# Both MLP products of a two-layer fp32 decoder as seven block products, with sums of weight blocks formed in DRAM by accumulating DMAs

## The chip, the cores and the metric

The kernel runs on one core of a Trainium2 chip. The metric is the device time of one execution in microseconds (us). Lower is better. Engines are named as the profile names them: PE (TensorE, the matrix engine), DVE (VectorE), ACT (ScalarE), POOL (GpSimd), SP (SyncE, which here only issues DMAs).

## The reference

One batch of 1024 tokens of 1024 features goes through two layers and a last RMSNorm, all in float32. The first layer mixes tokens by multi-head latent attention (MLA), the second by stick-breaking attention; each then has a cross-attention into 256 memory tokens and an MLP with 4096 hidden features:

```python
def sq_relu_mlp(h, w_in, w_out):
    return jnp.square(jax.nn.relu(h @ w_in)) @ w_out

def reference(x, mem, positions, ...):
    h = x
    for i in range(DEPTH):                       # DEPTH = 2
        a = rmsnorm(h, norm_mix[i])
        if i % 2 == 0: h = h + mla_mixer(a, cos, sin, ...)
        else:          h = h + stick_breaking_mixer(a, ...)
        h = h + mem_cross_attn(rmsnorm(h, norm_cross[i]), rmsnorm(mem, norm_mem[i]), ...)
        h = h + sq_relu_mlp(rmsnorm(h, norm_mlp[i]), mlp_w_in[i], mlp_w_out[i])
    return rmsnorm(h, norm_final)
```

## The kernel before

The residual stream `x` lies transposed in SBUF, features on partitions, as 16 tiles of 128 x 512: eight tiles of features for each of two chunks of 512 tokens. Every fp32 product is made of three passes in PE's faster format: an operand is split into `h` (rounded) and `l` (the rest), and `mm3` (L101 to L104) adds wh·xh, wh·xl and wl·xh into one PSUM bank. Weights come through `load_w` (L91 to L98): SP loads a raw block of 256 KB, ACT casts it to `h` (L97), POOL forms `l` (L89). Results leave PSUM through DVE or ACT.

Tiles are handed out from pools with a fixed number of slots for each tag, and a tile whose slots are all in use waits until one is free:

```python
SLOTS = dict(x=16, a=32, g=24, o=8, p=6, f=4, raw=3, w=8, pt=4, tmp=5)
PSLOTS = dict(s=3, pt=2, acc=3)
```

A scheduler orders the instructions of each engine by a simulated timeline; SP then issues all its DMAs in that order. A DMA queue has eight semaphores used in turn, so that an issue waits for the eighth DMA before it (`DMAHW..` in the order excerpts for SP's, `DMASW..` for POOL's).

The stages follow each other in time: MLA and the first cross-attention 0 to 617 us, the first MLP 617 to 1316, stick-breaking and cross-attention 1316 to 2037, the second MLP 2037 to about 2730, and then the last norm. In the attention stages `weave` (L257) emits two streams side by side: `self_attn` of one head, and as filling the projections of the next ones.

Before the MLP, `ready` takes each finished tile of `x`: it is multiplied by the gain alone and split (`gain_split`, tag `a`), and the statistics of the norm are gathered by `Norm`; `finish` of that class transposes and sums them (L138, L142) and spreads 1/rms over the partitions (L113, L114). Since 1/rms is a factor of each token, the first product of the MLP can begin without it: it is multiplied in when a bank is evicted (L854). Then the square of relu (L855) and the split of the result (L858, POOL). `win(f)` makes one f-tile of 128 hidden features for both chunks (2 x 8 k-tiles x 3 passes); after each four f-tiles ("a part", of eight) a product with four k-tiles of `w_out` is added onto `x` (`add_x`, L233). The last part of the second layer goes through `finish`, which also writes the output.

## Time and profile before

| | us |
|---|---|
| median of 3 runs | 2745.91 |
| lowest and highest run | 2743.05 and 2746.37 |
| profiled execution, its span | 2743.0 |
| PE busy | 2662.9 (97%) |
| DVE / POOL / ACT busy | 1373.9 / 1029.2 / 970.3 |
| the two MLP stages (617 to 1316, 2037 to 2743) | 699 and 706 |

The profiled execution's own time is its span, 2743.0 us, which is 2.9 us below the median of the runs. The page is read from the top: the busy shares name the engine that could bound the time, the slices say whether that holds in each stage, and the granted clock says whether PE ran at full speed. Then the waits of that engine say what is left besides its own work.

### The profile page before, as it was taken

Reading aid. Unit: us, or ns where it says so; the run is one execution under the profiler, and the core shown is the slowest. Engines: PE = TensorE matmul, PEld = TensorE weight load, DVE = VectorE, ACT = ScalarE, POOL = GpSimd, SP = SyncE. Lnnn points to the kernel's source line nnn. Section 1 sums busy time; section 2 is a strip of 40 time slices with the busy share of each in tenths; the row PEclk is TensorE's granted clock in tenths of the full one; section 3 lists DMA queues with packets and bytes.
Section 4 is the critical chain, followed back from the end, with each engine's and each line's share of the span. In section 5 each row is a group of like instructions: output and inputs, shape, how many; then the busy total and the mean of one; then the engine's idle time right before and its main releaser. Section 6 shows DMA issues by size and latency. Waiting matters only on the chain.

```text
span 2743.0 us, 34762 instructions
## 1 busy us (share of the span) xinstructions
PE 2662.9 (97%) x13446; PEld 2239.1 (82%) x13446; DVE 1373.9 (50%) x2504; ACT 970.3 (35%) x1956; POOL 1029.2 (38%) x788
## 2 busy tenths in 40 slices
PE   8899999999999999999999999999999999999997
PEld 6788889787888888888888888877878888888886
DVE  6777776874222222223475766687762222222227
ACT  7677676552111111112343333345531111111112
POOL 3543235544333333343423232246253333333332
PEclk9999999999999999999999999999999999999998
DMA  3000003111111111111111010122021111111111
GB/s 118 28 23 23 27 21 97 31 43 46 54 50 50 43 46 58 47 50 35 32 32 39 24 39 24 39 70 62 24 62 46 54 43 46 54 46 52 38 50 62
DMA packets 70164, 125.48 MB, mean 46 GB/s; under 512 B 7792, under 2 KB 12656, under 8 KB 70000
## 3 DMA queue, kind: packets, MB, share of 16 engines
q1 hardware_dynamic: 69856, 123.15, 15.1%
q8 instruction: 105, 1.72, 0.3%
q14 instruction: 59, 0.48, 0.1%
q10 hardware_dynamic: 144, 0.13, 0.0%
HBM read 119.05 MB, written 4.19 MB: 45 GB/s over the span
## 4 chain that ended last, share of the span: by engine, by line
PE 82%; DVE 12%; ACT 2%; issue 2%; POOL 1%; DMA 0%; SPq 0%; DVEq 0%; ACTq 0%; POOLq 0%
PE ps_acc L104 16%; PE ps_acc L103 16%; PE ps_acc L102 16%; PE ps_s L104 9%; PE ps_s L102 9%; PE ps_s L103 9%; PE ps_s L370 4%; DVE f L434 2%; PE ps_pt L392 2%; DVE a L192 2%; DVE p L439 1%; DVE x L233 1%; DVE tmp L131 1%; DVE tmp L181 1%; PE ps_s L775 1%
## 5 line engine op out<-in xcount | busy, mean ns | idle before, releaser
L89 POOL TENSOR_TENSOR w<-raw,w 128x512 fp32r<-128x512 f32 (+1 forms) x293 | 385.4, 1317 | 586.8 <-ACT w L97 567.0
L233 DVE TENSOR_TENSOR x<-ps_acc,x 128x512 f32<-128x512 f32 x408 | 278.1, 686 | 331.8 <-PE ps_acc L104 330.2
L97 ACT CAST w<-raw 128x512 fp32r<-128x512 f32 (+1 forms) x293 | 178.8, 611 | 438.4 <-PE ps_s L103 209.2
L102 PE MATMUL ps_acc<-a,w 128*128 128x512 f32 (+1 forms) x776 | 300.9, 388 | 10.1 <-DVE tmp L349 5.2
L104 PE MATMUL ps_acc<-a,w 128*128 128x512 f32 (+1 forms) x776 | 301.0, 388 | 1.0 <-POOL w L89 1.0
L103 PE MATMUL ps_acc<-a,w 128*128 128x512 f32 (+1 forms) x776 | 299.3, 386 | 1.6 <-DVE a L192 1.5
L89 POOL TENSOR_TENSOR g<-tmp,g 128x512 fp32r<-128x512 f32 x120 | 158.2, 1320 | 295.8 <-ACT g L184 237.3
L89 POOL TENSOR_TENSOR g<-pt,g 128x512 fp32r<-128x512 f32 x96 | 124.3, 1294 | 278.9 <-ACT g L858 278.9
L233 DVE TENSOR_TENSOR x<-ps_s,x 128x512 f32<-128x512 f32 x120 | 82.9, 691 | 228.1 <-PE ps_s L104 228.1
L858 ACT CAST g<-pt 128x512 fp32r<-128x512 f32 x96 | 59.5, 620 | 349.9 <-DVE pt L855 349.9
L102 PEld LDWEIGHTS ps_acc<-a,w 128*128 128x128 f32 x776 | 147.5, 190 | 39.7 <-DVE tmp L349 5.8
L854 DVE TENSOR_TENSOR pt<-ps_acc,tmp 128x512 f32<-128x512 f32 x64 | 44.1, 691 | 259.8 <-PE ps_acc L104 251.0
L103 PEld LDWEIGHTS ps_acc<-a,w 128*128 128x128 f32 x776 | 147.4, 190 | 31.9 <-DVE a L192 5.0
L104 PEld LDWEIGHTS ps_acc<-a,w 128*128 128x128 f32 x776 | 147.4, 190 | 30.1 <-POOL w L89 1.4
L89 POOL TENSOR_TENSOR p<-raw,p 128x512 fp32r<-128x512 f32 x73 | 97.2, 1331 | 175.6 <-ACT p L97 161.7
L854 DVE TENSOR_TENSOR pt<-ps_s,tmp 128x512 f32<-128x512 f32 x64 | 44.2, 691 | 236.9 <-PE ps_s L104 233.7
L104 PE MATMUL ps_s<-g,w 128*128 128x512 f32 (+1 forms) x378 | 148.2, 392 | 0.0
L102 PE MATMUL ps_s<-g,w 128*128 128x512 f32 (+1 forms) x378 | 148.0, 392 | 0.0
L103 PE MATMUL ps_s<-g,w 128*128 128x512 f32 (+1 forms) x378 | 148.0, 391 | 0.0
L102 PE MATMUL ps_acc<-g,f 128*128 128x512 f32 (+1 forms) x377 | 146.2, 388 | 0.0
L103 PE MATMUL ps_acc<-g,f 128*128 128x512 f32 (+1 forms) x377 | 146.2, 388 | 0.0
L104 PE MATMUL ps_acc<-g,f 128*128 128x512 f32 (+1 forms) x377 | 145.9, 388 | 0.0
(242 smaller groups left out, 7001.6 us busy)
## 6 DMA issues: line engine op xcount, KB each, us to landing
raw<-in_w_in SPq DMA_DIRECT2D x128, 256.0 KB, 2.6
raw<-in_w_out SPq DMA_DIRECT2D x128, 256.0 KB, 2.6
x<-in_xT SPq DMA_DIRECT2D x16, 256.0 KB, 5.1
raw<-in_w_mo SPq DMA_DIRECT2D x16, 256.0 KB, 2.7
raw<-in_w_xk SPq DMA_DIRECT2D x16, 256.0 KB, 2.7
raw<-in_w_xv SPq DMA_DIRECT2D x16, 256.0 KB, 2.7
raw<-in_w_xq SPq DMA_DIRECT2D x16, 256.0 KB, 2.6
raw<-in_w_xo SPq DMA_DIRECT2D x16, 256.0 KB, 2.6
```

Source lines behind the costliest of these rows:

```text
L89: eng.tensor_tensor(out=l, in0=full, in1=h.bitcast(F32), op=ALU.subtract)
L97: nc.scalar.copy(out=h, in_=raw)
L102: nc.tensor.matmul(out=ps, lhsT=wh, rhs=xh, start=start, stop=False, skip_group_check=True)
L103: nc.tensor.matmul(out=ps, lhsT=wh, rhs=xl, start=False, stop=False, skip_group_check=True)
L104: nc.tensor.matmul(out=ps, lhsT=wl, rhs=xh, start=False, stop=stop, skip_group_check=True)
L192: nc.vector.scalar_tensor_tensor(out=l, in0=xt, scalar=g, in1=h.bitcast(F32), op0=ALU.mult, op1=ALU.subtract)
L233: nc.vector.tensor_tensor(out=x[c][f], in0=ps, in1=x[c][f], op=ALU.add)
L370: nc.tensor.matmul(out=ps[:, :n], lhsT=lh, rhs=rh, start=(i == 0), stop=(i == len(passes) - 1), skip_group_check=True)
L392: nc.tensor.transpose(out=tp[:, o0:o0 + P], in_=col(probs[qi][kb // 4], kb % 4), identity=ident)
L434: nc.vector.tensor_tensor_scan(out=rev, data0=rev, data1=pt[j][:, :n], op0=ALU.mult, op1=ALU.bypass, initial=1.0 if j == len(pieces) - 1 e ...
L854: nc.vector.tensor_tensor(out=t, in0=ps, in1=r[c], op=ALU.mult)
L858: nc.scalar.copy(out=h, in_=t)
```

## The change

The matrices of each MLP are cut in two in both directions: the hidden product's tokens into the two chunks, its features into k-tiles 0 to 3 and 4 to 7, and the hidden features into parts. A product of 2 x 2 blocks is then made from seven block products instead of eight (Strassen's scheme, in Winograd's form), from four sums of weight blocks S1 to S4 and four sums of activation blocks T1 to T4. f-tiles 0 to 3 stay with the ordinary product; the other 28 form 14 pairs.

- **Weight sums.** `weight_sums(i)` forms S1 to S4 of both weight matrices of a layer in DRAM: `begin` copies a block (SP, L924 of the changed kernel), `add` adds another onto it by a DMA that accumulates (POOL's queue, L929). Each of the eight stages (begin S1, begin S3, add S1, begin S2 from S1, add S3, add S2, begin S4 from S2, add S4) has 12 DMAs of 7.34 MB together. They are emitted from `weave`, on two of three of its steps, in the layer's attention stage.
- **Entry.** For the MLP's norm `ready` now gathers the statistics first; when they are complete each tile is multiplied by gain and 1/rms (`normed`, DVE, tag `p`) and split (ACT, and DVE or POOL in turn). `quad(k)` forms T1 to T4 of the activations during the four ordinary f-tiles.
- **Input product.** `win` loads three raw weight tiles and four sums, splits all seven, and `seven` makes seven products of four k-tiles each in three PSUM banks, with an eviction (ACT or DVE) after each. The seven results that the next product needs, each 256 KB, are spilled to DRAM.
- **Output product.** `fetch` loads the seven tiles of a pair again and splits them; `wout` works on pairs 1, 2, 3, then 4 at a time, and 3, 2, 1 at the end, adds the results directly onto the tiles of `x`, and keeps one product (`p1`) per block until the end. The four ordinary f-tiles, also spilled, are reloaded and multiplied at the end.

Matmuls recorded before: 13446. The program of the change has 671 fewer.

```diff
+    def split(src, tag, eng):
+        w = src.shape[-1]
+        h, l = T(tag, F32R)[:, :w], T(tag, F32R)[:, :w]
+        nc.scalar.copy(out=h, in_=src)
+        split_l(l, src, h, eng)
+        return h, l
...
     def ready(c, f, gcol):
+        if gcol in (G_MLP, G_MLP + 8):
+            norm[c].add(x[c][f], nc.vector if f % 2 else nc.gpsimd)
+            if f == FT - 1:
+                rms[c], norm[c] = norm[c].finish(), Norm(D)
+                for k in range(FT):
+                    t = T("p")
+                    normed(t, c, k, gcol)
+                    act[c].append(split(t, "a", nc.vector if k % 2 else nc.gpsimd))
+            return
...
     def weave(main, fill):
         for n in mg:
+            turn[0] += 1
+            if turn[0] % 3 < 2:
+                next(aside[0], None)
...
+    def weight_sums(i):
...
+        def begin(name, src):
+            for key in keys:
...
+                tc.keep_in_program_order(nc.sync.dma_start(out=whole(name, *key), in_=src(*key)))
+                yield
+        def add(name, *src):
+            for key in keys:
+                tc.keep_in_program_order(nc.gpsimd.dma_start(out=whole(name, *key), in_=block(*key, *src),
+                                                             accum_op=ALU.add))
+                yield
...
+        yield from begin("S1", blk(1, 0))
+        yield from begin("S3", blk(0, 0))
+        yield from add("S1", 1, 1)
+        yield from begin("S2", other("S1"))
+        yield from add("S3", 1, 0)
+        yield from add("S2", 0, 0)
+        yield from begin("S4", other("S2"))
+        yield from add("S4", 0, 1)
+    def seven(a, b, n, psum, evict):
+        banks = [PS(psum) for _ in range(3)]
+        begun = set()
+        for (an, bn, j), ev in zip(SEVEN, evict):
+            wh, wl = a[an]
+            for k in range(n):
+                xh, xl = b[bn][k]
+                mm3(banks[j], col(wh, k), col(wl, k), xh, xl, j not in begun, k == n - 1)
+                begun.add(j)
+            ev(banks[j])
...
+        def win(n, kp):
...
+            for name, stage, tag, eng in (("A11", "raw", "w", po), ("S2", "p", "w", po), ("A12", "raw", "w", po),
+                                          ("S3", "p", "a", po), ("S1", "p", "a", po), ("A22", "raw", "a", po),
+                                          ("S4", "p", "a", po)):
+                t = T(stage)
...
+                nc.sync.dma_start(out=t, in_=src)
+                wa[name] = split(t, tag, eng)
...
+            seven(wa, b, 4, ("s", "acc")[n % 2], (e1, e2, e3, e4, e5, e6, e7))
...
+            for name, t in (("B11", g11), ("B21", g21), ("B22", g22), ("T1", t1), ("T3", g12), ("T2", t2), ("T4", t4)):
+                d = spilt[kp][name] = dram(f"{name}_{kp}")
+                nc.sync.dma_start(out=d, in_=t)
...
+        def fetch(kp):
+            r = ready_b[kp] = {}
+            for name, tag, eng in (("B11", "a", ve), ("T2", "g", po), ("B21", "a", ve), ("T3", "g", po),
+                                   ("T1", "g", ve), ("T4", "o", po), ("B22", "a", ve)):
+                t = T("tmp")
+                nc.sync.dma_start(out=t, in_=spilt[kp][name])
+                r[name] = split(t, tag, eng)
```

Where the change moves instructions, the order of the engines shows it at three places.

SP in the MLA stage, where the projections' weights are loaded. `uv`, `uqp`, `uk`, `uqn` and `mo` are weights of the MLA. Before:

```order
L95 DMA raw<-in_w_uv 128x512 [waits DMAHW4_49,Pool_49]
L95 DMA raw<-in_w_uqp 128x384 [waits DMAHW5_49,Pool_49]
L95 DMA raw<-in_w_mo 128x512 [waits DMAHW6_49,Pool_49]
L95 DMA raw<-in_w_mo 128x512 [waits DMAHW7_49,Pool_49]
L95 DMA raw<-in_w_uk 128x256 [waits DMAHW0_49,Pool_49]
L95 DMA raw<-in_w_uqn 128x384 [waits DMAHW1_49,Pool_49]
```

After, with S2 (`S_.._2789` and on) begun from the sums S1 (`S_.._1171` and on):

```order
L96 DMA raw<-in_w_uv 128x512 [waits DMAHW7_49,DMAHW4_49,Pool_49]
L96 DMA raw<-in_w_uqp 128x384 [waits DMAHW5_49,DMAHW0_49,Pool_49]
L924 DMA S_in_0_2789<-S_in_0_1171 32x4x2048 [waits DMAHW1_49,DMASW0_49]
L96 DMA raw<-in_w_mo 128x512 [waits DMAHW6_49,DMAHW2_49,Pool_49]
L924 DMA S_out_0_2848<-S_out_0_1221 32x2x2048 [waits DMASW1_49]
L924 DMA S_out_0_2888<-S_out_0_1242 32x2x2048 [waits DMASW2_49]
L924 DMA S_in_0_2961<-S_in_0_1280 32x4x2048 [waits DMASW3_49]
L924 DMA S_out_0_3008<-S_out_0_1306 32x2x2048 [waits DMASW4_49]
L96 DMA raw<-in_w_mo 128x512 [waits DMAHW7_49,Pool_49]
L924 DMA S_out_0_3110<-S_out_0_1369 32x2x2048 [waits DMAHW0_49,DMASW5_49]
L96 DMA raw<-in_w_uk 128x256 [waits DMAHW1_49,Pool_49]
L96 DMA raw<-in_w_uqn 128x384 [waits DMAHW2_49,Pool_49]
```

The loads of `w_mo` now stand behind copies that wait for POOL's accumulations (`DMASW`).

PE at the entry of the first MLP, where `ps_pt` with `ident` is the norm's chain and `ps_s<-a,w` (before also the `ps_acc<-a,w` here) the MLP's first product. Before, from inside that product:

```order
L104 MATMUL ps_s<-a,p 128x512
L102 MATMUL ps_acc<-a,w 128x512 [waits DVE_49]
L103 MATMUL ps_acc<-a,w 128x512
L113 MATMUL ps_pt<-ident,sm_y 128x128 [waits DVE_49]
L113 MATMUL ps_pt<-ident,sm_y 128x128 x3
L104 MATMUL ps_acc<-a,w 128x512
L102 MATMUL ps_acc<-a,w 128x512
L103 MATMUL ps_acc<-a,w 128x512
L138 MATMUL ps_pt<-ident,tmp 128x128 [waits DVE_49]
L138 MATMUL ps_pt<-ident,tmp 128x128 x3
L104 MATMUL ps_acc<-a,w 128x512
L102 MATMUL ps_acc<-a,w 128x512
```

After, with the cross-attention's last matmuls (`ps_acc`) at the top:

```order
L103 MATMUL ps_acc<-a,w 128x512
L104 MATMUL ps_acc<-a,w 128x512
L105 MATMUL ps_acc<-a,w 128x512
L114 MATMUL ps_pt<-ident,sm_y 128x128 [waits DVE_49]
L114 MATMUL ps_pt<-ident,sm_y 128x128 x3
L103 MATMUL ps_s<-a,w 128x512 [waits Activation_49]
L104 MATMUL ps_s<-a,w 128x512 [waits Pool_49]
L105 MATMUL ps_s<-a,w 128x512
L103 MATMUL ps_s<-a,w 128x512 [waits Activation_49]
L139 MATMUL ps_pt<-ident,tmp 128x128 [waits DVE_49]
L139 MATMUL ps_pt<-ident,tmp 128x128 x3
L104 MATMUL ps_s<-a,w 128x512 [waits DVE_49]
```

The norm's last small matmuls stood behind the beginning of the product, inside it, and now stand ahead of its first matmul, which waits for ACT.

SP in the MLP. Before, weights of both products in turn:

```order
L95 DMA raw<-in_w_in 128x512 [waits DMAHW0_49,Pool_49]
L95 DMA raw<-in_w_in 128x512 [waits DMAHW7_49,Pool_49]
L95 DMA raw<-in_w_in 128x512 [waits DMAHW1_49,Pool_49]
L95 DMA raw<-in_w_out 128x512 [waits DMAHW3_49,Pool_49]
L95 DMA raw<-in_w_out 128x512 [waits DMAHW2_49,Pool_49]
L95 DMA raw<-in_w_out 128x512 [waits DMAHW6_49,Pool_49]
L95 DMA raw<-in_w_out 128x512 [waits DMAHW5_49,Pool_49]
```

After, at the seam between the input and the output product, with spills of pairs (`B_`, `T_` as targets), reloads of pair 0 (`tmp<-`) and sums of `w_out` blocks (`f<-`):

```order
L1054 DMA B_13_0_10324<-tmp 128x512 [waits DMAHW4_49,Activation_49]
L1054 DMA B_13_0_10328<-f 128x512 [waits DMAHW5_49,Activation_49]
L1054 DMA B_13_0_10326<-pt 128x512 [waits DMAHW6_49,Activation_49]
L1086 DMA f<-S_out_0_2848 128x128 [waits DMAHW7_49,PE_49]
L1086 DMA f<-S_out_0_1666 128x128 [waits DMAHW0_49,PE_49]
L1054 DMA T_13_0_10330<-f 128x512 [waits DMAHW1_49,DVE_49]
L1054 DMA T_13_0_10332<-pt 128x512 [waits DMAHW2_49,DVE_49]
L1054 DMA T_13_0_10334<-tmp 128x512 [waits DMAHW3_49,DVE_49]
L1069 DMA tmp<-B_0_0_8140 128x512 [waits DMAHW4_49]
L1054 DMA T_13_0_10336<-tmp 128x512 [waits DMAHW5_49,DVE_49]
L1069 DMA tmp<-T_0_0_8150 128x512 [waits DMAHW6_49,PE_49]
L1069 DMA tmp<-B_0_0_8142 128x512 [waits DMAHW7_49]
```

The queue that held loads alone now has spills that wait for DVE and ACT, ahead of the first reloads.

## Rows read from the trace of the kernel before

**Rows 1.** The page, parts 1 (busy time, share, instructions) and 2 (busy tenths in 40 slices)

```profile
PE 2662.9 (97%) x13446; PEld 2239.1 (82%) x13446; DVE 1373.9 (50%) x2504; ACT 970.3 (35%) x1956; POOL 1029.2 (38%) x788
...
PE   8899999999999999999999999999999999999997
...
PEclk9999999999999999999999999999999999999998
```

**Rows 2.** PE's waits: engine, tile, line waited for; total us, times, longest us

```profile
PE ps_pt L113 <- DVE sm_y L151: 11.9, 8, 5.7
...
PE ps_s L102 <- ACT w L97: 7.4, 1, 7.4
...
PE ps_acc L102 <- DVE x L233: 4.8, 10, 1.0
```

**Rows 3.** The windows by stage, columns in the first row

```profile
core 0: us, PE busy (x) PEld busy (x) DVE busy (x) ACT busy (x) POOL busy (x), PEclk, DMA share, GB/s
...
617.00:1316.00 699.00, 696.00 (x3044) 571.25 (x3043) 204.16 (x298) 133.26 (x220) 253.58 (x198) 1.00 0.16 48
...
2037.00:2743.00 706.00, 686.13 (x3097) 566.80 (x3095) 219.29 (x352) 121.70 (x206) 244.49 (x190) 0.99 0.17 49
...
800.00:900.00 100.00, 100.00 (x439) 82.11 (x438) 25.71 (x36) 15.90 (x26) 33.29 (x26) 1.00 0.15 45
...
617.00:640.00 23.00, 20.00 (x86) 15.98 (x85) 15.91 (x36) 7.19 (x13) 9.54 (x8) 0.93 0.18 58
...
6.00:10.00 4.00, 2.50 (x5) 1.60 (x6) 2.61 (x3) 3.93 (x8) 2.61 (x3) 1.00 1.04 387
...
207.57:390.10 182.53, 181.83 (x1074) 158.98 (x1073) 131.60 (x306) 125.88 (x280) 69.31 (x57) 1.00 0.09 25
...
1496.44:1760.44 264.00, 254.26 (x1490) 220.91 (x1489) 174.38 (x289) 96.82 (x209) 74.13 (x57) 0.99 0.11 33
```

**Rows 4.** Groups by line and form: busy us, mean ns, idle us before and releasers

```profile
L89 POOL TENSOR_TENSOR w<-raw,w 128x512 fp32r<-128x512 f32 x273 | 366.1, 1343 | 549.0 <-ACT w L97 529.2 <-PE ps_acc L103 11.4 <-ACT o L167 7.9
...
L97 ACT CAST w<-raw 128x512 fp32r<-128x512 f32 x273 | 169.4, 621 | 423.7 <-PE ps_s L103 209.2 <-PE ps_acc L103 137.4 <-issue 68.7
...
L233 DVE TENSOR_TENSOR x<-ps_acc,x 128x512 f32<-128x512 f32 x408 | 278.1, 686 | 331.8 <-PE ps_acc L104 330.2
...
L855 DVE SCALAR_TENSOR_TENSOR pt<-pt 128x512 f32<-128x512 f32 x128 | 101.7, 796 | 4.1
```

**Rows 5.** Timeline of SP's DMA issues: start us, us, queue, line, tile, count

```profile
328.08 0.33 SPq L95 DMA_DIRECT2D raw<-in_w_uk  x1
...
390.10 30.46 SPq L699 DMA_DIRECT2D raw<-in_memT  x4
...
1755.10 4.48 SPq L95 DMA_DIRECT2D raw<-in_w_sq  x2
```

**Rows 6.** Timeline at the entry of the first MLP: start us, us, engine, instruction

```profile
627.44 1.10 PE L138 MATMUL ps_pt<-ident,tmp 128*128 128x128 f32 x4 [0.33 <-DVE tmp L131]
...
628.58 0.69 DVE L142 TENSOR_REDUCE sm_part<-ps_pt 128x32 f32<-128x512 f32 x1 [0.59 <-PE ps_pt L138]
...
638.66 0.60 PE L113 MATMUL ps_pt<-ident,sm_y 128*128 128x128 f32 x4
```

**Rows 7.** The page, part 6: DMA issues, KB each, median us to landing

```profile
raw<-in_w_in SPq DMA_DIRECT2D x128, 256.0 KB, 2.6
...
raw<-in_w_out SPq DMA_DIRECT2D x128, 256.0 KB, 2.6
```

**Rows 8.** Timeline of POOL, splits next to which accumulations come to stand

```profile
207.57 1.02 POOL L89 TENSOR_TENSOR w<-raw,w 128x384 fp32r<-128x384 f32 x1 [5.54 <-ACT w L97]
...
1496.44 1.42 POOL L89 TENSOR_TENSOR w<-raw,w 128x512 fp32r<-128x512 f32 x1
```

More of the change, by code (lines that the diff above doesn't have):

```diff
@@ L57, in trunk_kernel @@
     pp = ctx.enter_context(tc.tile_pool(name="pp", bufs=1, space=bass.MemoryType.PSUM))
+    dr = ctx.enter_context(tc.tile_pool(name="dr", bufs=1, space=bass.MemoryType.DRAM))
     def T(tag, dt=F32):
@@ L199, in trunk_kernel, with normed @@
     rms = [None, None]
+    def normed(t, c, f, gcol):
+        nc.vector.scalar_tensor_tensor(out=t, in0=x[c][f], scalar=gains[:, gcol + f:gcol + f + 1], in1=rms[c][1],
+                                       op0=ALU.mult, op1=ALU.mult)
     def ready(c, f, gcol):
+        if gcol in (G_MLP, G_MLP + 8):
[7 more added lines that the diff above has]
+            return
         h, l = T("a", F32R), T("a", F32R)
@@ L255, in stagger @@
                 unit(1, b - lag, ws.pop(b - lag))
+    aside, turn = [iter(())], [0]
     def weave(main, fill):
@@ L895, in trunk_kernel, with tt, rows @@
-    cross(0, *mla(G_CROSS), G_MLP)
-    mlp(0, G_MIX + 8)
-    cross(1, *stick(G_CROSS + 8), G_MLP + 8)
+    SEVEN = (("A11", "B11", 0), ("S2", "T2", 1), ("A12", "B21", 0), ("S3", "T3", 1), ("S1", "T1", 2), ("A22", "T4", 1),
+             ("S4", "B22", 2))
+    def tt(eng, out, a, b, op):
+        eng.tensor_tensor(out=out, in0=a, in1=b, op=op)
+    GROUPS = ((1, 4), (3, 4), (5, 4), (7, 2))
+    PAIRS = [(g, j) for g, (_, n) in enumerate(GROUPS) for j in range(n)]
+    def rows(w):
+        return w.rearrange("j (r a) c -> r j (a c)", a=4)
@@ new lines, in trunk_kernel, with w_in_blocks, w_out_block, block @@
+    sums = {}
+    def w_in_blocks(i, g, r, k):
+        p, n = GROUPS[g]
+        return ins["w_in"][i, 4 * p + n * r:4 * p + n * r + n, k]
+    def w_out_block(i, g, m, k):
+        p, n = GROUPS[g]
+        return ins["w_out"][i, p + k, m] if n == 4 else ins["w_out"][i, p, m][:, 2 * P * k:2 * P * k + 2 * P]
+    def weight_sums(i):
+        keys = [(kind, g, h) for g in range(len(GROUPS)) for kind, h in (("in", 0), ("out", 0), ("out", 1))]
+        def block(kind, g, h, r, k):
+            if kind == "in":
+                return rows(w_in_blocks(i, g, r, k))
+            p, n = GROUPS[g]
+            if n == 4:
+                return rows(ins["w_out"][i, p + k].rearrange("(h m t) p c -> h t m p c", t=2, h=2)[h, r])
+            w = ins["w_out"][i, p].rearrange("(h m t) p c -> h t p m c", t=2, h=2)
+            return w[h, r][:, :, 2 * P * k:2 * P * k + 2 * P]
+        def whole(name, kind, g, h):
+            t = sums[i, name, kind, g, h]
+            return rows(t) if kind == "in" or GROUPS[g][1] == 4 else t.rearrange("m p c -> p m c")
+        def begin(name, src):
+            for key in keys:
+                n = GROUPS[key[1]][1]
+                sums[i, name, *key] = dr.tile([n, P, C] if key[0] == "in" else [2, P, n * P], F32,
+                                              name=f"{name}_{key[0]}{key[1]}{key[2]}_{i}")
+                tc.keep_in_program_order(nc.sync.dma_start(out=whole(name, *key), in_=src(*key)))
[5 more added lines that the diff above has]
+                yield
+        def blk(*rk):
+            return lambda *key: block(*key, *rk)
+        def other(name):
+            return lambda *key: whole(name, *key)
+        yield from begin("S1", blk(1, 0))
[6 more added lines that the diff above has]
+        yield from add("S4", 0, 1)
@@ L898, in trunk_kernel @@
+    aside[0] = weight_sums(0)
+    kvm = mla(G_CROSS)
+    for _ in aside[0]:
+        pass
+    cross(0, *kvm, G_MLP)
+    mlp(0, G_MIX + 8)
+    aside[0] = weight_sums(1)
+    kvm = stick(G_CROSS + 8)
+    for _ in aside[0]:
+        pass
+    cross(1, *kvm, G_MLP + 8)
     mlp(1, None)
```

176 lines of the change are left out of this document (133 added, 43 removed).

## The prediction

> **What bounds the kernel now.** The page first: TensorE is busy 97% of the span of 2743.0 us, at its full clock in nearly every slice, and no other engine is busy over half [rows 1]. The list of what PE waits for comes next: its longest group is 11.9 us, and all 18 groups add to 70.6 us, of which three stand here [rows 2]. So the time is the number of matmuls times the interval between them. The windows give that interval and the room beside it, stage by stage: in the middle of the first MLP 439 matmuls start in 100.00 us, 0.228 us each, while DVE is busy 25.71 us of it, ACT 15.90 us, POOL 33.29 us and the DMA engines 15% [rows 3]. Both MLP stages together are 1405 us, PE busy 1382 us. A change can gain in two ways only: fewer matmuls, or fewer waits; waits are few, so the gain here is bounded by the matmuls that go, and everything else that the change brings can only cost, if it reaches PE.
>
> **What goes.** In 28 of 32 f-tiles of each MLP seven block products stand for eight: per product with the input weights 28 x 8 x 2 x 3 = 1344 matmuls become 14 steps x 84 = 1176, and the same for the output weights, so 336 per MLP and 672 in all. 672 x 0.228 = **-153 us**. The clock was granted in full there (1.00, the 2.4 GHz level [rows 3]) and should remain so, as PE stays busy.
>
> **Steady steps.** Per MLP there are 14 steps on the input and 14 full steps' worth on the output weights, 56 in all, each of 84 matmuls = 19.1 us of PE. Beside them must lie: on POOL 7 weight splits (input) or 7 and 3 of reloaded results (output), at 1.34 us [rows 4] 9.4 or 13.4 us; on ACT 14 to 16 casts and evictions at 0.62 us, about 9 to 10 us; on DVE five evictions at 0.69 us and four sums priced by the 0.80 us two-operand row [rows 4], 6.7 us, or seven evictions and four splits on the output side, about 8 us. DMA moves 14 blocks of 256 KB, 3.67 MB in 19.1 us = 192 GB/s, against 387 GB/s seen at the start [rows 3]; SP issues up to 21 at 0.33 us [rows 5] = 7 us. An accumulation returns to a PSUM bank after at least one other product, 12 x 0.228 = 2.7 us, and the eviction between takes 0.7 us. Every engine has room, so I take 0.2 us of waits a step, **+11 us**; bounds 0 and 30 (half a weight split in each step). The waits that the fewest slots (three for raw weights) could bring are a rival below.
>
> **Entry of the MLP.** Before, the raw tiles are split as they come, and 1/rms is applied at eviction: the order has PE in the product of the MLP (`ps_s<-a,w`) while the norm's small matmuls are still to come, and the trace shows that chain from 627.44 (L138) to 638.66 (L113), 11.2 us [rows 6], under running matmuls; the window 617 to 640 has PE busy 20.00 of 23.00 us at a mean clock of 0.93 [rows 3]. After, each split tile needs the norm first. The second order excerpt shows it: the norm's L114 stands directly ahead of the first `ps_s<-a,w`, whose matmuls then wait for ACT, POOL and DVE in turn. So per layer: the part of the chain not covered by the cross-attention's last products, up to 11.2 us; then one normed tile, cast and split (0.8 + 0.6 + 1.3 = 2.7 us); then eight tiles that DVE must make (12 of its operations, 8 x 0.8 + 4 x 0.7 = 9.2 us) against 24 x 0.228 = 5.5 us of PE for the first chunk, 3.7 us late. That is 11.2 + 2.7 + 3.7 = 17.6 us, less a little that other products cover: I take 15 a layer, **+30 us**; bounds 4 (chain covered) and 25 (clock at its 1.2 GHz level for some microseconds after the idle) a layer. The block sums of the activations (32 DVE operations, about 24 us; 16 POOL splits and 8 of weights, 32 us) lie beside 4 x 48 matmuls = 44 us.
>
> **Seam between the two products.** The results are spilled and come back by SP, whose third excerpt has the last spills of pair 13, each waiting for DVE, ahead of the first reloads. After the last matmul the eviction (0.7), two activations (1.2) and four sums (3.2) run, and about two landings of 2.6 us [rows 7], a cast and a split follow: roughly 4.3 + 2.6 + 0.6 = 7.5 us without PE work, then short steps (one, two, three pairs: products of 0.7 to 2 us against evictions of 0.7 us) and seven reloads through five `tmp` slots, as much again. I take 14 a layer, **+28 us**; bounds 8 and 25. The last short steps (3, 2, 1 pairs) and the reload of the four ordinary f-tiles: 4 a layer, **+8 us**, bounds 0 and 16.
>
> **The sums of weights, in attention.** Per layer 48 copies on SP and 48 accumulating DMAs on POOL, 29.4 MB each. PE's time is unchanged if they keep pace; they cost where SP, in order, stands at a copy that waits for an accumulation, with weight loads queued behind it, which POOL's splits and then PE wait for (first excerpt: `S_in_0_2789` waits for DMASW0, and `w_mo` is behind). The first accumulation stands just ahead of the split at 207.57 [rows 8]; the last copy of S4 stands ahead of the memory's loads at 390.10 [rows 5]. In these 182.5 us three of the four sums (22.0 MB of adds) must be done, with the S2 copies (7.34 MB) and 4.6 MB of loads (25 GB/s [rows 3]). Loads ran at 387 GB/s into SBUF; a copy both reads and writes, so I price it at half, 195 GB/s: 38 us, and the loads 12 us. That leaves 133 us, 166 GB/s. No row has an accumulating DMA. Bounds: 195 GB/s, as a copy (113 us, no loss); 100 GB/s, as four passes of 387 (220 us, 87 lost). I take the one that counts its transfers, two reads and a write, 387 / 3 = 130 GB/s: 169 us, 37 lost. In the second layer the stretch is 1496.44 [rows 8] to 1760.44, where the last copies of S4 stand, behind the issue at 1755.10 [rows 5]: 264 us; loads 8.7 MB (33 GB/s [rows 3]) 22 us, copies 38 us, 204 us left, 108 GB/s: at 130 nothing is lost, at 100 16 us; 5 us for loads that land behind copies on SP's queue. Together **+42 us**, bounds 0 and 108, or 220 if accumulations run at 80 GB/s. What POOL pays to issue one is not in the trace: between 0.33 us (SP's issue) and 1.3 us (a split), 48 a layer, 16 to 62 us in stretches where POOL is busy 69.31 of 182.53 and 74.13 of 264.00 us [rows 3]; I count it at nothing beside that idle time, and if the cover is gone it is in the upper bound.
>
> **Sum.** -153 + 11 + 30 + 28 + 8 + 42 = -34, so 2743.0 - 34 = 2709 for the profiled execution. The median of the runs is 2.9 us above its span: **2712 us**.
>
> **Rivals.** *Accumulations at or below 100 GB/s (slower).* The losses are 22.0 MB / rate - 133 and 22.0 MB / rate - 204 us, plus 5; they reach the 76 us at which the sum is zero at about 108 GB/s. At 100 they are 108 us: 2712 - 42 + 108 = 2778. For it: each such DMA needs three passes, POOL and SP both wait in order, and the first layer's stretch has little slack; against: the second layer has twice the slack, and the price is unseen. The Trainium skill bears on this (Collectives: The Full Stack, section "The bandwidth ceiling"): a reducing DMA runs at half the rate of a copying one, because it reads two sources. By that rule the sums here would come at 195 / 2 = 98 GB/s, an estimate, and the time would be this rival's; no run here shows an accumulation yet. *Splits arrive late in every step (about no change, or slower).* With three `raw` slots, a step's seven weight blocks can be loaded only as POOL frees them; if each of the 56 steps loses one split, 1.3 us, that is 73 instead of 11: 2774. Against: POOL has 6 to 10 us spare a step. *All covered (faster).* Seams at their lower bounds and DMAs as copies: -153 + 0 + 8 + 16 + 0 + 0 = -129: 2617. For it: so few waits in the trace now; against: the norm and the spill are chains that nothing else can fill. That the change removes fewer matmuls than it says is excluded by the order, which has 671 fewer.
>
> **How the numbers follow.** Forecast 0.50, slow accumulations 0.27, late splits 0.12, all covered 0.11. The forecast's own range is 2650 to 2760 (the terms' bounds do not all fall on one side). For 8 in 10 the range reaches down into the last case and up beyond the first rival's 2778: 2635 to 2825. About 0.2%, 5.5 us, is what a measurement can tell from no change. Faster: 0.44 of the forecast, 0.11, 0.03 of late splits, 0.02 of the slow sums: 0.60. Same: 0.07, from the forecast's upper end and both middle cases. Slower: 0.33.
>
> **What would show it.** Matmuls 12774; the MLP stages shorter by 153 us less 11 + 30 + 28 + 8 = 77, so 1405 to about 1329; the stages up to 617 and from 1316 to 2037 longer by 37 and 5. In the waits a group at the norm's L114 or the first `a` split of 10 to 17 us in each layer, and one on the first reload at the seam. If the first rival holds, the attention stages grow by over 76 us, PE waits for casts of weights, and SP's issues of copies span tens of microseconds. If splits are late, PE waits for POOL's `w` and `a` evenly through the MLP. The prediction is wrong if the accumulations cost PE nothing, or if their traffic slows loads long after they are issued.

## The result: half a per cent slower

| | before | after |
|---|---|---|
| median of the runs, us | 2745.68 | 2757.68 |
| runs, us | 2743.05 to 2746.37 | 2756.66 to 2767.62 |
| ratio, 95% interval | | 1.0051 [1.0034, 1.0068] |
| span of the profiled execution, us | 2743.0 | 2765.8 |

The forecast was 2712 us, faster; the kernel became slower by 12 us. The time lies inside the range, on the other side of no change. The profiled execution is 8 us longer than the median, and 22.8 us longer than the one of before. The following parts split up that difference of 22.8 us.

The page of after, parts 1 and 2 (as [rows 1]), and of part 3 the queue of POOL's accumulating DMAs (packets, MB, share of 16 engines):

```profile
PE 2574.7 (93%) x12774; PEld 2138.5 (77%) x12774; DVE 1640.6 (59%) x2754; ACT 1298.1 (47%) x2558; POOL 1389.3 (50%) x1098
...
PE   7897988898899989999999899989998999899997
...
PEclk9998999999899999999999999999999999999998
...
q0 software_dynamic: 12288, 58.73, 11.2%
```

The 672 matmuls are gone, and PE is busy 88 us less. But it is busy 93% of the span instead of 97%: in [rows 1] the first two slices and the last were below 9, now fourteen are. Each of these slices is 69 us long, and most of the new ones stand where the change put work beside PE. The stretches named ahead of the prediction (617 to 1316, 2037 to 2743) do not hold the two MLPs whole: in the trace of before, PE still works on the first one's output product at 1326, and the second one's first matmul starts at 2012.9, so the two are 1439.8 us, not 1405. The terms of the forecast are differences and do not hang on this. Cut at the last matmul of the cross-attention and at the norm behind the first MLP, the profiled executions have these stages (us; the kernels from x1 on are the experiments below, x2 and x3 with part of the computation changed):

```
                 first      first   second     second MLP
                 attention  MLP     attention  and end      span
before           617.0      709.7   686.2      730.1        2743.0
after            668.0      683.4   707.0      707.4        2765.8
x1_apart         638.2      682.9   702.1      707.9        2731.1
x2_plain         624.1      681.7   695.8      706.3        2707.9
x3_nosums        615.6      681.2   690.5      709.0        2696.3
x4_quad_dve      665.7      670.3   707.2      695.7        2738.9
x5_quad_reload   658.2      672.9   706.5      697.6        2735.2
x6_spread        640.3      684.0   697.7      705.5        2727.5
x7_seam          663.7      678.3   706.3      701.6        2750.0
x9_all_seam      638.7      657.8   696.6      684.4        2677.5
x10_memT         624.9      659.4   702.4      684.3        2671.0
```

(The expectations of the experiments cut a little later, at the norm's matmuls for the second chunk, 627.9 before and 677.1 after.)

The attention stages lost 51.0 and 20.8 us, together 71.8 where the forecast had 42. The MLP stages won 26.3 and 22.7 us, together 49.0 where 153 us of matmuls went; so they lost 104, where the forecast had 77.

The waits of PE over the whole of after (as [rows 2]):

```profile
PE ps_s L398 <- POOL g L90: 29.5, 4, 15.3
PE ps_s L103 <- ACT a L159: 21.5, 4, 8.7
PE ps_pt L114 <- DVE sm_y L152: 8.6, 6, 5.7
```

The first group is new: the scores of MLA wait for a split on POOL, 29.5 us in four waits, all in the first attention stage. The second is the MLP's: a reloaded result at the seam of its two products (17.3 us in two waits), and the first normed tile at its entry (4.2 us). The windows of the first MLP (columns as in [rows 3]) show where in it the time goes:

```profile
660.00:700.00 40.00, 31.25 (x118) 23.51 (x117) 36.75 (x61) 15.97 (x26) 20.86 (x14) 0.83 0.10 31
700.00:755.00 55.00, 43.79 (x165) 33.19 (x165) 46.22 (x39) 20.23 (x37) 44.86 (x28) 0.88 0.33 110
755.00:1010.00 255.00, 255.00 (x1105) 207.20 (x1104) 95.18 (x117) 125.00 (x209) 119.77 (x92) 1.00 0.58 181
1010.00:1050.00 40.00, 28.77 (x105) 20.34 (x104) 21.86 (x27) 20.73 (x43) 22.50 (x22) 0.87 0.73 238
```

From 755 to 1010 the steps of seven products run without a gap at the full clock (1.00, the 2.4 GHz level). What is lost is lost in three places of 40 to 55 us: the entry, the ordinary f-tiles beside which the block sums of the activations are formed (DVE busy 46.22 of 55 us), and the seam. In each, stretches at the 1.2 GHz level begin during or behind PE's idle time, so that the mean clock is 0.83 to 0.88.

PE's longest waits in the second and the third of these places, from its timeline in after:

```profile
733.84 0.77 PE L103 MATMUL ps_s<-a,w 128*128 128x512 f32 x1 [3.09 <-ACT w L159]
736.74 0.79 PE L105 MATMUL ps_s<-a,w 128*128 128x512 f32 x1 [1.70 <-POOL w L90]
744.76 0.80 PE L103 MATMUL ps_s<-g,w 128*128 128x512 f32 x1 [3.63 <-ACT w L159]
...
1027.45 0.80 PE L103 MATMUL ps_s<-a,w 128*128 128x512 f32 x1 [8.57 <-ACT a L159]
```

The first three stand in the first step of seven products, right behind the ordinary f-tiles: PE waits there for the cast and the split of that step's weights, on engines that still work on the block sums. Between the entry and that step it waits only 1.5 us in all.

### The profile page after: what moved, and what is told of

The parts are those of the page before. It is cut to its first block, busy times and chain, and to the rows that moved or that the text cites. A ratio compares the mean times of both kernels' runs of the same rounds, so it can differ in the third digit from the quotient of the medians.

```text
span 2765.8 us, 37140 instructions
## 1 busy us (share of the span) xinstructions
PE 2574.7 (93%) x12774; PEld 2138.5 (77%) x12774; DVE 1640.6 (59%) x2754; ACT 1298.1 (47%) x2558; POOL 1389.3 (50%) x1098
## 3 DMA queue, kind: packets, MB, share of 16 engines
q0 software_dynamic: 12288, 58.73, 11.2%
## 4 chain that ended last, share of the span: by engine, by line
PE 64%; DVE 13%; DMA 4%; issue 2%; POOL 2%; ACT 2%; SPq 0%; DVEq 0%; POOLq 0%; ACTq 0%
PE ps_acc L103 13%; PE ps_acc L104 13%; PE ps_acc L105 13%; PE ps_s L103 7%; PE ps_s L104 7%; PE ps_s L105 7%; DVE p L212 2%; DVE f L462 2%; PE ps_s L398 1%; DVE p L879 1%; DVE x L256 1%; DVE p L467 1%; POOL w L90 1%; PE ps_pt L420 1%; DMA raw<-in_w_xv 1%
## 5 line engine op out<-in xcount | busy, mean ns | idle before, releaser
L90 POOL TENSOR_TENSOR w<-raw,w 128x512 fp32r<-128x512 f32 (+3 forms) x313 | 415.1, 1341 | 478.0 <-ACT w L98 338.5
L98 ACT CAST w<-raw 128x512 fp32r<-128x512 f32 (+2 forms) x189 | 114.2, 605 | 238.3 <-PE ps_acc L104 149.8
L103 PE MATMUL ps_s<-a,w 128*128 128x512 f32 (+1 forms) x416 | 169.1, 406 | 37.7 <-ACT a L159 21.5
L90 POOL TENSOR_TENSOR a<-p,a 128x512 fp32r<-128x512 f32 x100 | 137.0, 1375 | 102.7 <-ACT a L159 81.9
L398 PE MATMUL ps_s<-g 128*128 128x512 f32 (+3 forms) x576 | 141.1, 359 | 36.0 <-POOL g L90 29.5
L104 PE MATMUL ps_s<-a,w 128*128 128x512 f32 (+1 forms) x416 | 168.6, 405 | 5.5 <-POOL a L90 2.3
L105 PE MATMUL ps_s<-a,w 128*128 128x512 f32 (+1 forms) x416 | 166.9, 402 | 4.5 <-POOL w L90 4.5
L90 DVE TENSOR_TENSOR a<-tmp,a 128x512 fp32r<-128x512 f32 x92 | 90.9, 993 | 134.2 <-ACT a L159 133.3
L90 DVE TENSOR_TENSOR pt<-ps_pt,pt 128x512 fp32r<-128x512 f32 (+1 forms) x192 | 122.2, 639 | 67.8 <-ACT pt L176 67.1
L176 ACT CAST pt<-ps_pt 128x512 fp32r<-128x512 f32 (+1 forms) x192 | 104.9, 554 | 87.8 <-PE ps_pt L420 46.0
L103 PE MATMUL ps_acc<-o,w 128*128 128x512 f32 x304 | 129.1, 425 | 11.5 <-DVE x L256 8.5
L398 PEld LDWEIGHTS ps_s<-g 128*128 128x128 f32 x576 | 95.6, 192 | 51.3 <-POOL g L90 30.7
```

The source lines that it names most:

```text
L90: eng.tensor_tensor(out=l, in0=full, in1=h.bitcast(F32), op=ALU.subtract)
L98: nc.scalar.copy(out=h, in_=raw)
L103: nc.tensor.matmul(out=ps, lhsT=wh, rhs=xh, start=start, stop=False, skip_group_check=True)
L104: nc.tensor.matmul(out=ps, lhsT=wh, rhs=xl, start=False, stop=False, skip_group_check=True)
L105: nc.tensor.matmul(out=ps, lhsT=wl, rhs=xh, start=False, stop=stop, skip_group_check=True)
L176: nc.scalar.copy(out=h, in_=ps)
```

## Where POOL stood in attention

The timeline of POOL in after, around the longest wait (start, duration, what; the idle time before and what ended it in brackets), and the matmul that waited:

```profile
240.38 1.15 POOL L929 DMA_DIRECT2D S_out<-in_w_out  x1 [6.65 <-issue]
254.29 1.15 POOL L929 DMA_DIRECT2D S_out<-in_w_out  x1 [12.76 <-DMA S_out<-S_out]
255.01 2.66 POOL L90 TENSOR_TENSOR w<-raw,w 128x384 fp32r<-128x384 f32 x2
257.18 1.70 POOL L90 TENSOR_TENSOR g<-tmp,g 128x512 fp32r<-128x512 f32 x1
...
258.94 0.80 PE L398 MATMUL ps_s<-g 128*128 128x512 f32 x1 [15.35 <-POOL g L90]
```

POOL stands at two accumulating DMAs from 233.7 to 254.29, but for the issue at 240.38. Two weight splits and the split of `g` are behind them in its order, and PE waits 15.35 us for the latter. The page guesses what ended POOL's wait from the semaphores of the instruction; the landings say something else. An accumulation moves pieces of 8 KB, or of 1 KB where a group has only two pairs (the last two DMAs of each sum); counted in pieces, those under way at each late issue are:

```
kernel     issued  own     under way  same, with  a landing   under way
           at us   pieces  before it  own pieces  ended at    after issue
after      240.38  256     320        576         240.02      448
after      254.29  256     256        512         253.96      256
after      349.93  256     256        512         349.60      256
after      415.99  256     256        512         415.66      256
x1_apart   218.72   64     448        512         218.47      256
x1_apart   230.97  256     256        512         230.64      448
x1_apart   240.82   64     448        512         240.56      384
```

("before it" is before that landing.) In after, nine accumulations were issued within 0.45 us of the landing that brought the sum under 512, in x1_apart seventeen (two and one of them with no idle time of POOL before), and among all 96 of each kernel no issue left more than 448 pieces under way. The eight semaphores that a queue uses in turn are not the reason: where such an issue had an eighth DMA before it, that one had landed 15.6 us or more ahead (at 218.91 and 225.43 for the issues at 240.38 and 254.29). That is how the stand was read; the experiments were made to test it.

**x1_apart** changes only the order of the twelve DMAs within each sum:

```diff
         keys = [(kind, g, h) for g in range(len(GROUPS)) for kind, h in (("in", 0), ("out", 0), ("out", 1))]
+        keys = keys[:2] + keys[10:11] + keys[2:7] + keys[11:] + keys[7:10]
```

> Same copies and accumulations; only the order of the twelve DMAs of a sum differs: the two with 256 pieces of 1 KB each (last pair group of the output weights) stand five DMAs apart instead of next to each other at the end. Theory A (POOL stands still): in the changed kernel the second of the two is issued 0.33 us after the first has landed, POOL's splits queue behind it, and PE waits 29.5 us for them in four waits, with 17.1 and 13.7 us at half clock after the longest. Then these waits go and MLA shortens by 25 to 45 us: 2715 to 2735. Rival B (accumulations are slow as such): the bytes and the rate are the same, so the time stays at 2750 to 2765 and the waits move to other places.

Measured: 2735.39 us, ratio to before 0.997 [0.996, 0.998], at the upper end of what theory A gave. PE's waits for POOL's `g` in MLA fell from 29.5 us in four to 2.7 us in one:

```profile
PE ps_s L398 <- POOL g L90: 2.7, 1, 2.7
```

The first attention stage fell from 668.0 to 638.2 us. Theory A held for the waits; 22.6 us more than in x3_nosums remain, and POOL still stood, up to 8.4 us at a time (ahead of the issue at 230.97 in the table).

**x2_plain** leaves `accum_op` away, so that the same DMAs on the same queue copy:

```diff
-                tc.keep_in_program_order(nc.gpsimd.dma_start(out=whole(name, *key), in_=block(*key, *src),
-                                                             accum_op=ALU.add))
+                tc.keep_in_program_order(nc.gpsimd.dma_start(out=whole(name, *key), in_=block(*key, *src)))
```

> The accumulating DMAs are plain copies of the same blocks on the same queue, in the changed kernel's order, so the sums are not formed. Rival B (accumulation is what is slow): the attention stages lose their 70 us or most of them, 2690 to 2715. Theory A: the stand of POOL stays, only as much shorter as the first of the two DMAs lands sooner; 2740 to 2757.

Measured: 2709.19 us, 0.9871 [0.9855, 0.9887]. This went the rival's way: theory A had expected the stand to stay. The queue's line of x2_plain:

```profile
q0 software_dynamic: 9216, 58.73, 6.2%
```

The same 58.73 MB take 6.2% of the engines instead of 11.2%. Over the spans that is 168 against 310 us with all 16 engines, or 350 against 190 GB/s, a factor of 1.85. A part of it is the size of the packets: the trace has the accumulated pieces of 1 KB as 4096 packets, and the copied ones as 1024 packets of 4 KB. The pieces of 8 KB are packets of 8 KB in both, 0.67 us each against 0.37 us, a factor of 1.81. And POOL never stood before an issue, though up to 704 pieces were under way, counted as in the table; counted by packets the most was 512, at one issue. So the limit below 512 pieces was met by accumulations alone; that one of them takes more room in the queue than a copied piece is likely, but rests on this count. The two theories are not alternatives: accumulations land later, and POOL stands while too many are under way. The Trainium skill (Collectives: The Full Stack, section "The bandwidth ceiling") puts the reducing step of a collective at half the rate of its copying step, with a measured ratio of 1.93, because the add needs two source reads. The 1.81 to 1.85 here are near it.

**x3_nosums** forms no sums at all and lets the MLP load plain weight blocks where sums stood:

```diff
-    aside[0] = weight_sums(0)
...
-    aside[0] = weight_sums(1)
...
-                    src = sums[i, name, "in", gr, 0][j]
+                    src = w_in_blocks(i, gr, int(name[1]) % 2, int(name[1]) // 3)[j]
...
-                        src = sums[i, name, "out", gr, mp // 2][mp % 2]
+                        src = w_out_block(i, gr, m + int(name[1]) % 2, int(name[1]) // 3)
```

> No copies and no accumulations; the MLP loads plain weight blocks where the sums stood, so that its DMAs, splits and matmuls are as many as before. The product is then another one. All theories: the attention stages fall back to the lengths they had before the change (MLA's 47.8 us and stick-breaking's 17 us go), 2685 to 2695. If the MLP stages get shorter as well, the sums' traffic or late landings cost there too; I expect them to stay at 674.6 and 656.8 us.

Measured: 2697.92 us, 0.983 [0.9813, 0.9846], just above the 2685 to 2695 expected, with attention stages of 615.6 and 690.5 us and MLP stages within 2.2 us of after's. The sums cost 2757.7 - 2697.9 = 60 us. By x2_plain 11 us of it are the copies and the traffic; 48 us are there only when the DMAs accumulate. In the second attention stage the sums cost 707.0 - 690.5 = 16.5 us; PE has no waits for POOL's `g` there, and no experiment finds what takes them.

**x6_spread** lets accumulations alternate with copies, on top of x1_apart (excerpt):

```diff
-        yield from add("S1", 1, 1)
-        yield from begin("S2", other("S1"))
-        yield from add("S3", 1, 0)
+        for _ in zip(add("S1", 1, 1), begin("S3", blk(0, 0))):
+            yield
+            yield
+        for _ in zip(begin("S2", other("S1")), add("S3", 1, 0)):
+            yield
+            yield
...
```

> As x1_apart, and the accumulations stand in turn with copies, one of two or two of three, instead of twelve in a row. In the changed kernel and in x1_apart no accumulation was issued while 512 or more pieces would have been under way (448 at most), and nine and seventeen were issued within 0.45 us of the landing that brought the sum below 512. Theory A (POOL stands when the queue has no room): with at most two or three under way the stands go, the stages up to 627.9 before end at 628 to 638 instead of 647.3: 2715 to 2726. Rival (what is left in x1_apart is the traffic's): as x1_apart, 2730 to 2740.

Measured: 2732.72 us, 0.9957 [0.9942, 0.9972], above the 2715 to 2726 expected and where the rival put it, but not for its reason: POOL's stands were gone (none over 1.5 us), and another wait had come in their place. ACT, SP and PE in x6_spread:

```profile
393.31 0.54 SPq L925 DMA_DIRECT2D S_out<-S_out  x1
393.94 0.57 SPq L727 DMA_DIRECT2D raw<-in_memT  x1
...
410.69 0.42 ACT L128 ACTIVATE a<-raw 128x256 f32<-128x256 f32 x1 [15.64 <-DMA raw<-in_memT]
...
412.84 1.33 PE L420 MATMUL ps_pt<-ident,p 128*128 128x128 f32 x5 [12.09 <-ACT p L452]
```

A load of the memory stands on SP's queue behind a copy of 256 pieces, issued 0.6 us before. The copy landed at 408.83, the load at 410.67, 16.7 us after its issue (2.4 us in x3_nosums); ACT stands at it with the softmax behind it, and PE waits 12.09 us. The trace's packets show the order on SP's queue: the copy's 256 packets of 1 KB run from 397.46 to 407.87, and the load's 128 packets of 2 KB from 407.46 to 410.38, on the 16 engines together. Beside them POOL's queue has packets of 8 KB, 0.66 us each, while one of the copy's takes 0.07 us.

**x10_memT** is all that helped (x9_all_seam, below), with these loads on ACT's queue:

```diff
-                nc.sync.dma_start(out=raw, in_=ins["memT"][b])
+                nc.scalar.dma_start(out=raw, in_=ins["memT"][b])
```

> As x9_all_seam, with the memory's raw loads (8 in the kernel) on ACT's queue instead of SP's. In x6_spread and x9_all_seam the first of them landed 16.7 us after its issue in x6_spread, 2.4 us in x3_nosums; on SP's queue a copy of 256 pieces stands just ahead of it, and ACT, then PE (12.1 and 12.6 us) wait for it. If the place behind the copy on SP's queue is the cause, it lands within some 8 us, that wait goes and the MLA stage gets 10 to 18 us shorter with the half clock behind it: 2668 to 2677. If the DMA engines are full of accumulations whatever the queue, it still lands after 12 us or more: 2682 to 2690.

Measured: 2675.14 us, 0.9745 [0.9729, 0.9762]. The first of the loads now lands 4.4 us after its issue, the wait is gone, and the first attention stage is 624.9 instead of 638.7 us (the second is 5.8 us longer, and the median gains 10.5). With the packets above, the place behind the copy on SP's queue was the cause, as expected. But the edit moved the load in time as well: it is issued at 390.39 and landed at 394.79, and the copy is issued at 394.06. So it passed while accumulations in 1 KB pieces were on the engines, ahead of those in 8 KB pieces, which run from 395 us on; what the other queue alone is worth was not measured.

## The block sums of the activations, and the seam

**x4_quad_dve** moves the splits of the block sums from POOL to DVE, the engine that was the busier one:

```diff
-                b[name].append(split(t, tag, po))
+                b[name].append(split(t, tag, ve))
```

> The splits of the activations' block sums go from POOL to DVE, 16 a layer. In the changed kernel DVE is busy 43.40 of the 45 us from 700 to 745, its two-operand operations taking either 0.68 or about 1.75 us. Theory C (the long ones are those that overlap POOL's splits): with the splits on DVE most operations take 0.7 us, 16 more of them cost 11 us and about 32 shorter ones save 1.0 us or less each; the stage gets 2 to 8 us shorter a layer, 2742 to 2754. Rival D (the durations belong to the operation): DVE has 16 x 1.2 = 19 us more a layer and the stage grows by as much, 2785 to 2800.

Measured: 2739.18 us, 0.9983 [0.9969, 0.9997]; the MLP stages got 13.1 and 11.7 us shorter, more than theory C expected. The groups of DVE by line in after, then in x4_quad_dve (busy us, mean ns, idle us before):

```profile
L212 DVE SCALAR_TENSOR_TENSOR p<-x,gains,tmp 128x512 f32<-128x512 f32 x64 | 73.9, 1192 | 2.7 <-ACT tmp L115 2.7
L879 DVE TENSOR_TENSOR p<-p 128x512 f32<-128x512 f32 x32 | 40.4, 1271 | 0.3
```

```profile
L212 DVE SCALAR_TENSOR_TENSOR p<-x,gains,tmp 128x512 f32<-128x512 f32 x64 | 65.0, 1048 | 2.0 <-ACT tmp L115 2.0
L879 DVE TENSOR_TENSOR p<-p 128x512 f32<-128x512 f32 x32 | 23.6, 747 | 0.0
```

The same sums take 747 ns instead of 1271. In after, of 32 of them the six that overlap no POOL operation take 0.68 to 0.69 us each; of the 26 that lie more than half beside one, 18 take 1.65 to 1.78 us and eight 0.68. Here is one such stretch of after, DVE and then POOL:

```profile
692.96 0.68 DVE L90 TENSOR_TENSOR a<-p,a 128x512 fp32r<-128x512 f32 x1
693.56 1.78 DVE L212 SCALAR_TENSOR_TENSOR p<-x,gains,tmp 128x512 f32<-128x512 f32 x1
695.26 0.68 DVE L90 TENSOR_TENSOR a<-p,a 128x512 fp32r<-128x512 f32 x1
```

```profile
693.10 1.69 POOL L90 TENSOR_TENSOR a<-p,a 128x512 fp32r<-128x512 f32 x1 [1.27 <-ACT a L159]
```

The operation that meets POOL's split ends only about 0.6 us after it; its neighbours take 0.68. So a split on POOL costs DVE up to 1.1 us if DVE has two operands in SBUF. The Trainium skill states this (SBUF — State Buffer, section "SBUF: two separate sides"): the two engines share a port pair, which the first to start holds for the whole instruction. The trace agrees, with 0.68 against 1.78 us, and the rule was not weighed in the prediction.

**x5_quad_reload** spills the normed tiles and reloads them, so that DVE need not make them twice:

```diff
                     normed(t, c, k, gcol)
+                    nrm[c, k] = dr.tile([P, C], F32, name=f"n{c}{k}_{gcol}")
+                    nc.sync.dma_start(out=nrm[c, k], in_=t)
...
-                normed(t, c, f, gcol)
+                nc.sync.dma_start(out=t, in_=nrm[c, f])
```

> The normed tiles of the entry are spilled and reloaded for the activations' block sums, so that DVE makes 16 operations a layer instead of 32 there and SP 32 DMAs more. If DVE's load is what PE waits for in the ordinary f-tiles (17.8 and 16.4 us lost there in the changed kernel), 16 x 1.2 = 19 us go from DVE and most of that loss: 10 to 14 us a layer, 2730 to 2738. If the splits on POOL bound it (34.86 of 45 us busy), no more than 5 us a layer: 2748 or more.

Measured: 2741.02 us, 0.999 [0.998, 1.0], somewhat above the 2730 to 2738 expected. The MLP stages got 10.5 and 9.8 us shorter. The windows of the ordinary f-tiles in x4_quad_dve, then in x5_quad_reload, to be held against 700 to 755 of after:

```profile
698.00:753.00 55.00, 50.78 (x212) 40.23 (x211) 45.63 (x58) 25.96 (x47) 26.30 (x18) 0.97 0.44 141
```

```profile
690.00:745.00 55.00, 50.33 (x212) 40.38 (x211) 36.77 (x25) 26.44 (x48) 52.08 (x34) 0.97 0.67 214
```

PE has 212 matmuls instead of 165 in 55 us either way. With the splits on DVE it is DVE that stays the busiest, with 45.63 us for 58 operations instead of 46.22 for 39; with the reload it is POOL, with 52.08 us. So the loss there was not one engine's load: both were busy over 80% of those 55 us in after, and each slowed the other.

**x7_seam** emits the reloads of the first pair ahead of the last pair's sums and spills (excerpt):

```diff
+            if kp == len(PAIRS) - 1:
+                fetch(0)
             g21, g12, g22 = p1, u2, u3
...
-            if t < len(pairs):
+            if 0 < t < len(pairs):
                 fetch(pairs[t])
```

> The reloads of the first pair are emitted ahead of the last pair's sums and spills. If the order of SP's queue sets the seam (the first reload was issued 23.77 - 18.65 = 5.1 us after PE's last matmul), it shrinks from about 19 and 9 us to 12 and 5: 2744 to 2752. If the free slots and the short first steps set it, no change: 2754 to 2760.

Measured: 2751.3 us, 1.0028 [1.0015, 1.0041]; the MLP stages got 5.1 and 5.8 us shorter. That is about a quarter of the seam's loss. The wait of 8.57 us for the first reload is gone, and half of it comes back as a wait for the cast of a weight:

```profile
1018.51 0.50 PE L103 MATMUL ps_s<-g,w 128*128 128x512 f32 x1 [4.12 <-ACT w L159]
```

The rest of the loss, the short steps behind the seam, stays.

**x9_all_seam** is x4, x5, x6 and x7 together:

> x4_quad_dve, x5_quad_reload, x6_spread and x7_seam together. If their causes are separate, their gains add: from 2757.7, the accumulations' 30 to 40, the block sums' 24 to 34, the seam's 5 to 10: 2675 to 2700. If one cause lies under several (a stage that another resource bounds next), less: 2700 to 2720.

Measured: 2685.64 us, 0.9785 [0.9771, 0.98]. Singly they gained 18.5, 16.7, 25.0 and 6.4 us, 66.6 in all; together 72.0. In the ordinary f-tiles of the first MLP and the first step behind them PE's loss is now 0.5 us (17.8 in after, 6.4 and 7.0 in x4 and x5). With x10_memT's one line more the change makes the kernel 2.55% faster than before it. Parts 1 and 2 of the page of x10_memT:

```profile
PE 2551.1 (96%) x12774; PEld 2126.6 (80%) x12774; DVE 1603.6 (60%) x2754; ACT 1297.6 (49%) x2558; POOL 1333.1 (50%) x1066
...
PE   8899999898999999999999999989999999899997
...
PEclk9999999998999999999999999999889999999998
```

Seven slices are still below 9, four more than before the change. The norm and the first tiles at the entry, and at the seam the wait for the cast of a weight (4.25 us in x10_memT), are waits that none of the experiments takes away.

## Why the prediction was wrong, point by point

Losses inside a stage are summed here over PE's matmuls in the trace of after, as the time from start to start beyond 0.228 us.

- **What goes.** Right: 12774 matmuls, 153 us at the interval of [rows 3].
- **Steady steps**, 11 us. Right: 12.6 us over both layers.
- **Entry**, 30 us. Right in size, 13.6 + 13.9 = 27.5 us, but partly by luck, as the parts are others. The norm's chain, counted with up to 11.2 us a layer, lay almost wholly under the cross-attention's last products: PE waited 0.38 us for it. The forecast did not have a second round for the second chunk's norm and first tile, and had only in a bound what fell to the 1.2 GHz level here, stretches of 10.2 and 3.4 us a layer. PE's waits at the entry of the first MLP in after:

```profile
668.56 0.65 PE L114 MATMUL ps_pt<-ident,sm_y 128*128 128x128 f32 x4 [0.38 <-DVE sm_y L152]
671.32 0.51 PE L103 MATMUL ps_s<-a,w 128*128 128x512 f32 x1 [2.11 <-ACT a L159]
673.12 0.79 PE L104 MATMUL ps_s<-a,w 128*128 128x512 f32 x1 [1.29 <-POOL a L90]
676.63 1.11 PE L139 MATMUL ps_pt<-ident,tmp 128*128 128x128 f32 x4 [1.86 <-DVE tmp L132]
678.30 0.79 PE L104 MATMUL ps_s<-a,w 128*128 128x512 f32 x1 [0.56 <-DVE a L90]
685.59 0.65 PE L114 MATMUL ps_pt<-ident,sm_y 128*128 128x128 f32 x4 [0.44 <-DVE sm_y L152]
688.36 0.73 PE L103 MATMUL ps_acc<-a,w 128*128 128x512 f32 x2 [2.11 <-ACT a L159]
```

- **The block sums beside the ordinary f-tiles**, nothing. Wrong: 17.8 + 16.4 = 34.2 us, about two thirds of it in the first step behind them, whose weights' casts and splits stood behind the block sums. This term was hidden by adding up each engine's operations at the prices of [rows 4] and finding less than 44 us on each. The 24 us of DVE left out the squares, and the normed tiles of the second chunk that fall into the same stretch; and the prices were those of operations measured apart, 0.69 and 0.80 us, where DVE's took 1.19 and 1.27 us beside POOL's splits (x4_quad_dve).
- **Seam**, 28 us. Mis-sized: 19.2 + 18.1 = 37.3 us, still inside its bounds. PE's last matmul before it begins at 1018.49 and the first behind it at 1027.45, 8.7 us beyond the interval, and the ramp behind it was the larger part. The 7.5 us forecast for the gap do not follow from the parts named with it: 0.7 + 1.2 + 3.2 are 5.1 us, not 4.3, and two landings of 2.6 us, a cast of 0.6 and a split of 1.3 would make 12.2.
- **Tail**, 8 us. Nothing to be seen, 1.0 and -1.3 us. And some 8 us of waits that the MLP stages had before are gone, which the sum had not counted.
- **The sums of weights**, 42 us. Mis-sized, 71.8 as the attention stages of the profiled execution grew, 60 by the medians of after and x3_nosums, and the step that gave it failed: the price was put on the rate at which accumulations finish (130 GB/s taken) and on SP, standing at copies. SP did stand there, 51.6 us from 200 to 500 us and up to 10.9 at a time, but PE waited only 3.5 us for casts and splits of weights in that attention stage. At the 190 GB/s that the queue's line gives, that working would have found nothing lost, 22.0 MB / 190 = 116 us in 133. The loss came from POOL, which had been given 0.33 to 1.3 us an issue and idle time as cover: it stands while an issue would bring its accumulations under way to 512 pieces or more, and the splits of activations stand behind it. The prediction named POOL's waiting in its rival, but put no price of its own on it; the trace of before showed POOL busy only 69.31 of 182.53 us [rows 3], which says nothing about who is queued behind an issue that waits.
- **The rival of slow accumulations** is what the sum came to resemble, 2757.7 against the 2778 it gave, and for its reason only in part: accumulating is slower than copying, by 1.85, but at 190 and not at 100 GB/s. That late splits of the block sums and a longer seam would add to it was not foreseen. **Late splits in every step** did not happen. **All covered** was out of reach for the change as it stood; x10_memT, at 2675, is a little more than half of the way from after to its 2617.

So the sign hung on two terms of some 30 us, each of which counted time on an engine and not what stands behind it there. Of the 51.0 us in the first attention stage, PE was idle for 40.6 more than before (67.0 against 26.4 us), 29.5 of them the waits for POOL; the other 10.3 us are the same 3320 matmuls being busy longer, 26.4 us of them at the 1.2 GHz level against 10.2 before. What stays open are the other 11 us of idle time, and the 20.8 us of the second attention stage. The attention stage of kernels that share its code (after, x4, x5, x7) lay between 658.2 and 668.0 us, so a few us of any single difference there are the execution's own.

## What to carry to other kernels

A DMA that is issued from a working engine costs that engine more than its issue when too much of its queue is under way: list what stands behind the issue in that engine's order, and keep few pieces under way. Price two engines that work side by side on SBUF from a stretch where they did so, not from each one's mean. And look at a load's place on its queue: behind one copy in small pieces, with accumulations beside it, a load landed 14 us later than without, and PE waited 12 us for it.

## What was not expected of the hardware

- Accumulating DMAs issued by POOL never had more than 448 pieces under way, and an issue that would have made it 512 or more waited for a landing; plain copies of the same shapes reached 704 without a wait (512 by the packets that the trace has for them).
- Accumulation took 1.85 times the DMA engines' time of a copy of the same bytes (11.2% of 2765.8 us against 6.2% of 2707.9); packets of 8 KB took 0.67 against 0.37 us.
- A copy in DRAM of 256 pieces of 1 KB, 256 KB in all, landed 15.5 us after its issue while accumulations ran, and the load behind it on the same queue 1.8 us later; its packets ran only behind the copy's.
- Idle times of PE at the entry, in the f-tiles and at the seam came with stretches of 3.4 to 10.2 us at the 1.2 GHz level, in attention of up to 17.1 us, which began during the idle time or behind it: after spent 150 us there, 105 of them with PE busy, and before 20.5, all busy, each without the last 20 us of its span.
